# Loading one block in three smaller transfers at the moment when the first store joins a saturated load queue

## Chip, cores, metric

One core of one Trainium2 chip. The metric is device time in microseconds (us) of one execution, median over runs. The profiled span is about 1.7 us shorter than the time of the same run (316.3 against 318.03 for the kernel before).

## Reference

```python
# x: (8, 1024, 2048) float32, gamma: (2048,), eps: scalar
rms = np.sqrt(np.mean(x ** 2, axis=-1, keepdims=True) + eps)
out = gamma * x / rms
return out * (1 / (1 + np.exp(-out)))      # SiLU
```

The 8192 rows of 8 KB are read once and written once: 67.1 MB each way.

## The kernel before

Rows are taken in 16 blocks of 512. A block is a tile of 128 partitions with 4 rows (32 KB) each, so a block is one transfer of 128 contiguous runs of 32 KB. Loads go out on the SyncE queue (q1 in the profile), stores on the ScalarE queue (q10). There are six block buffers; block `b + 6` is loaded when the store of block `b` has landed.

```python
    def load(b):
        xt = pool.tile([P, J * d], f32, name="xt")          # J = 4 rows per partition
        nc.sync.dma_start(out=xt, in_=xb[b])
        blocks[b] = xt
    # ... sums: squares of two rows on ACT, of two on DVE; the store of an earlier
    # ... block is issued on ACT after the first of its squares
    def store(b):
        nc.scalar.dma_start(out=ob[b], in_=blocks[b])
        if b + LEAD < nblk:                                  # LEAD = 6
            load(b + LEAD)
    # ...
        grow = pool.tile([P, J * d], f32, name="xt")         # the sixth buffer, for gamma
        for b in range(BUFS - 1):                            # loads 0 to 4
            load(b)
        # ... constants, gamma load on the ScalarE queue, gamma broadcast by matmul
        load(BUFS - 1)                                       # load 5
        sums(0); invert(0); finish(0)
        sums(1); invert(1)
        for b in range(1, last - 1):
            sums(b + 1, after_first=[b - 1])                 # store b-1 goes out here
            finish(b)
            invert(b + 1)
        # ... the last block is stored in two halves
```

Of the kernel before, what the change touches and what calls it, by code (L numbers as in the profile page):

```python
# [1 line left out]

# [4 lines left out]

ACT = mybir.ActivationFunctionType
ALU = mybir.AluOpType


@with_exitstack
def kernel(
    ctx: ExitStack,
    tc: tile.TileContext,
    x: bass.AP,
    gamma: bass.AP,
    eps: bass.AP,
    out: bass.AP,
):  # L20





    nc = tc.nc
    P = nc.NUM_PARTITIONS
    f32 = mybir.dt.float32
    x2 = x.flatten_outer_dims()
    o2 = out.flatten_outer_dims()  # L30
    n, d = x2.shape
    J = 4
    BUFS, LEAD = 6, 6
    nblk = n // (P * J)
    xb = x2.rearrange("(b p j) d -> b p (j d)", p=P, j=J)
    ob = o2.rearrange("(b p j) d -> b p (j d)", p=P, j=J)

    singles = ctx.enter_context(tc.tile_pool(name="singles", bufs=1))
    pool = ctx.enter_context(tc.tile_pool(name="pool", bufs=BUFS))
    small = ctx.enter_context(tc.tile_pool(name="small", bufs=2))  # L40
    psum = ctx.enter_context(tc.tile_pool(name="psum", bufs=1, space=bass.MemoryType.PSUM))

    g = singles.tile([P, d], f32)
    eps_t = singles.tile([P, 1], f32)
    ones = singles.tile([P, P], f32)
    junk_a = psum.tile([P, d], f32, name="junk_a")
    junk_v = psum.tile([P, d], f32, name="junk_v")
    blocks, rmss, rstds = {}, {}, {}

    def load(b):  # L50
        xt = pool.tile([P, J * d], f32, name="xt")
        nc.sync.dma_start(out=xt, in_=xb[b])  # L52
        blocks[b] = xt

    def row(b, j):
        return blocks[b][:, j * d:(j + 1) * d]

    def sums(b, after_first=()):


        ss = small.tile([P, J], f32, name="ss")
        na = J // 2
        for j in range(na, J):
            nc.vector.tensor_tensor_reduce(  # L64
                out=junk_v, in0=row(b, j), in1=row(b, j), scale=1.0, scalar=0.0,
                op0=ALU.mult, op1=ALU.add, accum_out=ss[:, j:j + 1])
        for j in range(na):
            nc.scalar.activation(out=junk_a, in_=row(b, j), func=ACT.Square,  # L68
                                 accum_out=ss[:, j:j + 1])
            if j == 0:  # L70
                for s in after_first:
                    store(s)
        rms = small.tile([P, J], f32, name="rms")
        nc.scalar.activation(out=rms, in_=ss, func=ACT.Sqrt, scale=1.0 / d, bias=eps_t)  # L74
        rmss[b] = rms

    def invert(b):
        rstd = small.tile([P, J], f32, name="rstd")
        nc.vector.reciprocal(out=rstd, in_=rmss.pop(b))  # L79
        rstds[b] = rstd  # L80

    def finish(b, halves=False):
        for j in range(J):
            nc.vector.scalar_tensor_tensor(out=row(b, j), in0=row(b, j), scalar=rstds[b][:, j:j + 1],  # L84
                                           in1=g, op0=ALU.mult, op1=ALU.mult)
            if j % 2:
                cols = slice((j - 1) * d, (j + 1) * d)
                nc.scalar.activation(out=blocks[b][:, cols], in_=blocks[b][:, cols], func=ACT.Silu)  # L88
                if halves:
                    nc.scalar.dma_start(out=ob[b][:, cols], in_=blocks[b][:, cols])  # L90

    def store(b):
        nc.scalar.dma_start(out=ob[b], in_=blocks[b])  # L93
        if b + LEAD < nblk:
            load(b + LEAD)

    with tc.manual_schedule():


        Q = 4  # L100
        w = d // Q
        grow = pool.tile([P, J * d], f32, name="xt")
        for b in range(BUFS - 1):
            load(b)
        nc.vector.memset(ones, 1.0)  # L105
        nc.vector.memset(eps_t, float(eps))  # L106
        nc.scalar.activation(out=junk_a[:, 0:1], in_=ones[:, 0:1], func=ACT.Square)  # L107
        nc.scalar.dma_start(out=grow[0:P:P // Q, 0:w],
                            in_=bass.AP(tensor=gamma.tensor, offset=gamma.offset, ap=[[w, Q], [1, w]]))
        for c in range(Q):  # L110
            k = c * (P // Q)
            nc.tensor.matmul(junk_v[:, c * w:(c + 1) * w], ones[k:k + 1, :], grow[k:k + 1, 0:w],  # L112
                             start=True, stop=True)
        nc.vector.tensor_copy(out=g, in_=junk_v)  # L114
        load(BUFS - 1)


        last = nblk - 1
        sums(0)
        invert(0)  # L120
        finish(0)
        sums(1)
        invert(1)
        for b in range(1, last - 1):
            sums(b + 1, after_first=[b - 1])
            finish(b)
            invert(b + 1)
        store(last - 2)
        finish(last - 1)
        store(last - 1)  # L130
        sums(last)
        invert(last)
        finish(last, halves=True)


# [1 line left out]
_INS = ['x', 'gamma', 'eps']  # L137
_OUTS = [((8, 1024, 2048), 'float32')]

_NUMBERS = {'eps': 9.999999747378752e-06}  # L140


# [26 lines left out]
```

## Time and profile before

| | kernel before |
|---|---|
| time, median | 317.5 us (317.49 to 317.79, 3 runs) |
| DVE, ACT busy | 71%, 71% |
| load queue, store queue, share of 16 engines' time | 49.7%, 49.2% |
| 32 KB packet | 1.213 us |
| first load packet starts; last packet ends | 1.7 us; 314.9 us |

The transfer engines' row of the slices and the two queue shares say what binds here. The page, the table by stretches and the chain are quoted in the prediction.

A *packet* is one record of one transfer engine in the trace; here it is one contiguous run (32, 16 or 8 KB), and each transfer ends on each engine with a *landing packet* of 4 bytes, which counts its landing. The records don't name the engine, so I followed the packets by their times, each to the one that starts where it ends (16 chains per trace). The *loss at the join* is, per engine, what the time from one packet's start to the next exceeds the usual for its size, summed from 30 us to just after the first large store packet; figures are means over the 16 engines unless said otherwise.

All times below are counted from the start of the profiled span, as on the page and in the timeline. The packet times in the prediction and in the expectations are not: they are counted from a fixed point of the trace that lies 0.40 us ahead of the span's start in this profile. So 0.40 us is to be taken off the packet times there ("first store packet at 41.4 us", "ends at 313.76"). The losses are differences and are not touched by it. The expectations give some losses up to 0.07 us differently from the table, from an earlier count.

### The profile page before, as it was taken

How to read it: one execution, taken by the hardware profiler on the slowest of the kernel's cores; microseconds unless marked ns; L12 is line 12 of the kernel's file. 1: busy time of each engine (PE TensorE's matmuls, PEld its weight loads, DVE VectorE, ACT ScalarE, POOL GpSimd, SP SyncE). 2: the span in 40 equal slices, each digit the busy share in tenths (PEclk: the TensorE clock that was granted, in tenths of full speed). 3: DMA queues.
4: the chain of work that ended last, by engine and by line, in shares of the span. 5: the costliest groups of instructions: out<-in, count | busy, mean ns of one | idle time of the engine just before them, and what ended most of it. 6: DMA issues, size and time to landing. Idle time of an engine off the chain costs nothing.

```text
span 316.3 us, 444 instructions
## 1 busy us (share of the span) xinstructions
PE 2.1 (1%) x8; PEld 0.5 (0%) x8; DVE 223.5 (71%) x147; ACT 223.8 (71%) x144; POOL 0.2 (0%) x4
## 2 busy tenths in 40 slices
PE   0200000000000000000000000000000000000000
PEld 0000000000000000000000000000000000000000
DVE  0679499999493983939849397593966939993900
ACT  1357958999967777678676687676786776879540
POOL 0000000000000000000000000000000000000000
DMA  8999999999999999999999999999999999999996
GB/s 328 402 464 410 452 390 410 452 419 443 439 424 452 411 452 410 452 414 456 406 456 414 448 414 448 439 423 452 414 452 410 452 414 456 406 456 410 452 407 269
DMA packets 4763, 134.25 MB, mean 425 GB/s; under 512 B 532, under 2 KB 532, under 8 KB 536
## 3 DMA queue, kind: packets, MB, share of 16 engines
q1 hardware_dynamic: 2304, 67.11, 49.7%
q10 hardware_dynamic: 2456, 67.12, 49.2%
q14 instruction: 3, 0.02, 0.0%
HBM read 67.12 MB, written 67.11 MB: 424 GB/s over the span
## 4 chain that ended last, share of the span: by engine, by line
DMA 74%; DVE 14%; ACT 5%; issue 2%; DVEq 1%; ACTq 0%; SPq 0%
DMA xt<-in_x_dram 44%; DMA out_dram<-xt 30%; DVE xt L84 11%; ACT xt L88 3%; DVE junk_v L64 3%; ACT junk_a L68 1%; DVEq L164 1%; ACT L74 0%; ACT rms L74 0%; DVE rstd L79 0%; ACTq L93 0%; DVE ss L64 0%; SPq L52 0%; DVEq L64 0%; ACTq L74 0%
## 5 line engine op out<-in xcount | busy, mean ns | idle before, releaser
L84 DVE SCALAR_TENSOR_TENSOR xt<-xt,rstd,g 128x2048 f32<-128x2048 f32 x64 | 146.2, 2347 | 0.1
L88 ACT ACTIVATE xt<-xt 128x4096 f32<-128x4096 f32 x32 | 115.4, 3615 | 36.8 <-DVE xt L84 36.7
L64 DVE CUSTOM_DVE_ANT_0 junk_v<-xt 128x2048 f32<-128x2048 f32 x32 | 73.5, 2298 | 56.1 <-DMA xt<-in_x_dram 55.5
L68 ACT ACTIVATE junk_a<-xt 128x2048 f32<-128x2048 f32 x32 | 60.1, 1879 | 29.2 <-DMA xt<-in_x_dram 28.3
L74 ACT ACT_TABLE_LOAD x15 | 19.2, 1283 | 9.9 <-DVE ss L64 9.9
L88 ACT ACT_TABLE_LOAD x15 | 19.2, 1283 | 3.1 <-DVE xt L84 2.9
L79 DVE RECIPROCAL rstd<-rms 128x4 f32<-128x4 f32 x16 | 2.8, 172 | 11.3 <-ACT rms L74 11.3
L114 DVE COPY g<-junk_v 128x2048 f32<-128x2048 f32 x1 | 2.3, 2292 | 9.2 <-PE junk_v L112 9.2
L68 ACT ACTIVATION_READ_ACCUMULATOR junk_a<-xt 128x1 f32 x32 | 6.0, 186 | 0.0
L74 ACT ACTIVATE rms<-ss,eps_t 128x4 f32<-128x4 f32 x16 | 4.8, 297 | 1.2 <-DVE ss L64 1.1
L64 DVE DVE_READ_ACCUMULATOR2_ANT ss<- 128x1 f32 x32 | 4.5, 141 | 0.0
L112 PE MATMUL junk_v<-xt,ones 1*128 1x512 f32 x8 | 2.1, 1133 | 8.1 <-DMA xt<-in_gamma_dram 8.1
L107 ACT ACT_TABLE_LOAD x1 | 1.3, 1283 | 0.7 <-PEq L150 0.7
L105 DVE MEMSET ones<- 128x128 f32 x1 | 0.2, 165 | 0.8 <-PEq L150 0.8
L112 PEld LDWEIGHTS junk_v<-xt,ones 1*128 1x128 f32 x8 | 0.5, 306 | 8.1 <-issue 8.1
L107 ACT ACTIVATE junk_a<-ones 128x1 f32<-128x1 f32 x1 | 0.2, 174 | 0.0
L150 POOL MEMSET const-uint8-127<- 128x1 uint8 x1 | 0.1, 102 | 0.0
L150 POOL MEMSET const-bfloat16-1.0<- 128x1 bf16 x1 | 0.1, 101 | 0.0
L150 POOL MEMSET const-float32-0.0<- 128x1 f32 x1 | 0.1, 98 | 0.2 <-issue 0.2
L150 POOL MEMSET const-float32-1.0<- 128x1 f32 x1 | 0.1, 98 | 0.0
L106 DVE MEMSET eps_t<- 128x1 f32 x1 | 0.1, 59 | 0.0
## 6 DMA issues: line engine op xcount, KB each, us to landing
xt<-in_x_dram SPq DMA_DIRECT2D x16, 4096.0 KB, 42.0
out_dram<-xt ACTq DMA_DIRECT2D x15, 4096.0 KB, 35.2
out_dram<-xt ACTq DMA_DIRECT2D x2, 2048.0 KB, 10.4
xt<-in_gamma_dram ACTq DMA_DIRECT2D x1, 8.0 KB
```

The source lines that it names most:

```text
L64: nc.vector.tensor_tensor_reduce(out=junk_v, in0=row(b, j), in1=row(b, j), scale=1.0, scalar=0.0, op0=ALU.mult, op1=ALU.add, accum_out=ss[ ...
L68: nc.scalar.activation(out=junk_a, in_=row(b, j), func=ACT.Square, accum_out=ss[:, j:j + 1])
L74: nc.scalar.activation(out=rms, in_=ss, func=ACT.Sqrt, scale=1.0 / d, bias=eps_t)
L79: nc.vector.reciprocal(out=rstd, in_=rmss.pop(b))
L84: nc.vector.scalar_tensor_tensor(out=row(b, j), in0=row(b, j), scalar=rstds[b][:, j:j + 1], in1=g, op0=ALU.mult, op1=ALU.mult)
L88: nc.scalar.activation(out=blocks[b][:, cols], in_=blocks[b][:, cols], func=ACT.Silu)
L105: nc.vector.memset(ones, 1.0)
L107: nc.scalar.activation(out=junk_a[:, 0:1], in_=ones[:, 0:1], func=ACT.Square)
L112: nc.tensor.matmul(junk_v[:, c * w:(c + 1) * w], ones[k:k + 1, :], grow[k:k + 1, 0:w], start=True, stop=True)
L114: nc.vector.tensor_copy(out=g, in_=junk_v)
L150: nc = _bacc.Bacc("TRN2", target_bir_lowering=False, num_devices=1)
L164: with _tile.TileContext(nc) as tc:
```

## The change

The intent: when the first store (store 0, issued at 36.7 us) joins, the engines shall be working on 8 KB load packets instead of 32 KB ones, so that the store gets in sooner. Block 3 is the block in flight then.

```diff
-    def load(b):
+    def load(b, cuts=(0, 4)):
         xt = pool.tile([P, J * d], f32, name="xt")
-        nc.sync.dma_start(out=xt, in_=xb[b])
+        for c0, c1 in zip(cuts, cuts[1:]):
+            c = slice(c0 * d, c1 * d)
+            nc.sync.dma_start(out=xt[:, c], in_=xb[b][:, c])
         blocks[b] = xt
 ...
-        for b in range(BUFS - 1):
+        for b in range(3):
             load(b)
 ...     (constants and gamma load, unchanged)
+        load(3, cuts=(0, 2, 3, 4))
+        load(4)
```

## The prediction

> **What bounds the kernel now.** I read the busy shares first, then the slices and the queues, then the table by stretches, then the chain, and last the tail of the timeline.
>
> The page of the kernel before:
>
> ```profile
> span 316.3 us, 444 instructions
> PE 2.1 (1%) x8; PEld 0.5 (0%) x8; DVE 223.5 (71%) x147; ACT 223.8 (71%) x144; POOL 0.2 (0%) x4
> ...
> DMA  8999999999999999999999999999999999999996
> ...
> q1 hardware_dynamic: 2304, 67.11, 49.7%
> q10 hardware_dynamic: 2456, 67.12, 49.2%
> ```
>
> DVE and ACT are busy 71% of the span; the sixteen transfer engines are at 9 in every slice but the first and the last. The two queues (q1 loads, q10 stores) hold 49.7 + 49.2 = 98.9% of all engine time. A packet is a whole row of a block: 2304 packets of q1 are 16 loads x 128 rows of 32 KB plus 16 x 16 small ones that count the landing. So the kernel is bound by moving 134.2 MB, and only the remaining 1.1% or a better rate is to be won.
>
> The table by stretches shows where the rate falls short:
>
> ```profile
> 2.00:36.00 34.00, 2.09 (x8) 0.55 (x8) 20.95 (x14) 17.56 (x14) 0.00 (x0) 1.00 0.98 421
> 36.00:44.00 8.00, 0.00 (x0) 0.00 (x0) 5.70 (x6) 6.85 (x10) 0.00 (x0) 1.00 1.00 385
> 44.00:64.00 20.00, 0.00 (x0) 0.00 (x0) 19.97 (x13) 16.19 (x11) 0.00 (x0) 1.00 1.01 437
> 64.00:150.00 86.00, 0.00 (x0) 0.00 (x0) 64.15 (x44) 68.13 (x45) 0.00 (x0) 1.00 1.00 433
> 150.00:278.00 128.00, 0.00 (x0) 0.00 (x0) 94.61 (x61) 92.90 (x58) 0.00 (x0) 1.00 1.00 432
> ```
>
> The last two columns are the transfer engines' share and GB/s. From 64 us on the rate is 432 to 433 GB/s; in the 8 us in which the first store joins it is 385 although the engines count as fully busy: packets take longer there. I therefore went to the single packets of the trace. A 32 KB packet takes 1.213 us, load or store, nearly everywhere; on one engine packets follow each other without a gap, and load and store packets alternate strictly one by one whenever both queues have work. Two places stick out. The first packet of each engine, at 2.1 us, is 0.77 us too long on average. And around 38 to 42 us, after the first store is issued, one or two load packets of each engine are too long, together 0.85 us on average (0.55 at the least, 1.51 at the most), after which the first store packet follows at 41.2 to 43.3 us. All the rest of the run has 0.15 us of such excess on average. So the sum of the span is: 2.1 us until the first packet, (2048 + 2048) x 1.213 / 16 = 310.5 us of packets, 0.77 + 0.85 + 0.15 = 1.8 us of excess, which makes 314.4; the worst engine ends at 315.3 (it has the 1.51 us of excess at the join, and 1 us of other hiccups), most at 313.7; then about 1 us of ending.
>
> The chain and the timeline at the join and in the tail:
>
> ```profile
> 36.67 24.75 DMA out_dram<-xt
> ...
> 61.49 41.87 DMA xt<-in_x_dram
> ```
> ```profile
> 36.67 0.36 ACTq L93 DMA_DIRECT2D out_dram<-xt  x1
> ...
> 52.13 2.27 DVE L64 CUSTOM_DVE_ANT_0 junk_v<-xt 128x2048 f32<-128x2048 f32 x1
> ...
> 55.81 0.34 ACTq L93 DMA_DIRECT2D out_dram<-xt  x1
> ```
> ```profile
> 285.68 0.34 ACTq L93 DMA_DIRECT2D out_dram<-xt  x1
> ...
> 300.25 0.34 ACTq L90 DMA_DIRECT2D out_dram<-xt  x1
> ...
> 304.77 0.34 ACTq L90 DMA_DIRECT2D out_dram<-xt  x1
> ```
>
> The first store takes 24.75 us: about 4.5 until its first packet, 18.2 for eight packets per engine alternating with loads (7 x 2.426 + 1.213), and the landing. In the tail, the half stores are issued at 300.25 and 304.77 us, but the packets show the store before them running until about 304.3 us and the first half until about 309.1. So there is about 4 us of slack ahead of the last stores: the end is set by the transfers, and a microsecond won or lost anywhere in the transfers goes straight to the end.
>
> **What the Trainium skill says.** "DMA: Bandwidth & Descriptors", section "Queues, rings and completion order": each engine takes turns between the queues it has work for, packet by packet, draining a whole packet from one before switching. The trace agrees, with L, S, L, S at 1.213 us each; it differs in that a packet here is one descriptor of 32 KB, not some nine to seventeen descriptors. The same page, "Issuing engines are not separate DMA queues": transfers issued from different engines run on the same 16 engines and interleave; the 49.7% and 49.2% agree. The same page, "Where 436 GB/s comes from", gives 435 GB/s as the ceiling of the ports: the trace's 432 to 433 is at it, so no split of a transfer can raise the plateau.
>
> **The change part by part.**
> 1. Block 3 becomes a transfer of 16 KB rows and two of 8 KB rows. Each engine then has 8 packets of 16 KB and 16 of 8 KB instead of 8 of 32 KB. The two last stores have 16 KB packets of 0.611 us, against 1.213 for 32 KB: a fixed part of 0.009 us and 0.602 per 16 KB, hence, an estimate, 0.310 us for 8 KB. 24 packets instead of 8 cost 16 x 0.009 = 0.14 us per engine, and two more landing packets 0.02: **+0.16 us**, on the bound.
> 2. Two more issues on the load queue, 0.33 us each by the timeline's issue times; the queue is filled tens of us ahead: 0. The gamma load is written ahead of loads 3 and 4, but goes out on another queue, at the same place of ACT's order: 0.
> 3. The program uses eight landing semaphores in turn. With two more transfers ahead, load 5 must wait, besides for the release of its buffer (about 10 us), for load 1's landing (22.8 us) as it reuses its semaphore. Load 5's packets don't start until after 60 us: 0.
> 4. Which packets are under way at the join. Load 3 starts at 32.0 us: 8 x 0.611 = 4.9, so the 8 KB rows begin at 36.9, just when the store is issued (36.67), and alone would last until 41.9. The change is aimed well. The first store packets wait behind fewer bytes, so I expect them at 38.5 to 40.5 us instead of 41.3. From there the strict alternation gives the store 32 KB against 8 KB: a pair takes 1.213 + 0.310 = 1.52 us, eight pairs 12.2 us. The first store's packets end at about 51 to 52 us and it lands at 52 to 53.5, a landing 8 to 9 us earlier than at 61.4. Load 6 is issued that much earlier, but behind loads 4 and 5: no gain, since bytes moved per time are the same. Load 3 lands at 52 to 53 instead of 45; DVE wants it at 52.13, so it waits up to 1.5 us, which costs nothing as DVE is not the bound.
> 5. What the join costs. The excess of 0.85 us falls on load packets of 1.2 us. If it is a share of the packet in progress, 8 KB packets bring it to about a quarter, say -0.6 us; if it is a fixed delay of starting the store queue, it stays. I take **-0.3 us**.
> 6. A second join. Store 1 is issued at 55.8 us, because ACT comes to it only then, whatever store 0 does. The store queue, which in the kernel before is never empty after 41 us, now runs dry from about 52 to 60 us; loads have the engines alone, with 32 KB packets, and store 1 joins into those. If joining an empty queue costs 0.85 us each time, it is paid here in full; if only the first use of the queue costs, nothing. Half: **+0.4 us**.
> By 61 us the same bytes are moved in both kernels, load and store queues stand as before within a packet, and the steady part is the same. Sum: 0.16 - 0.3 + 0.4 = about +0.2 us, within the noise of 317.49 to 317.79: I predict 317.6 us.
>
> **Rivals.**
> - The split does what it is meant to: join excess gone to a quarter, also on the slowest engine (1.51 to 0.4), and the second join is free. For it: the long packets are exactly the 32 KB load packets before the first store packet. Then -0.6 to -1.1 + 0.16: 316.6 to 317.0 us.
> - The cost is moved, not removed: the first join as long as before or the second pays the same. For it: the start of the load queue at 2.1 us shows the same 0.77 us of excess without any other queue beside it, so it looks like the cost of starting a queue. Against: nothing in the trace shows a queue restarted. Then 317.7 to 318.6.
> - A new wait: the late landing of load 3 holds DVE, load 5 waits for load 1. Against: tens of us of slack in the load queue, and 29% idle DVE. Only if store 1's issue went far beyond 56 us and loads 4 and 5 ran out would the engines idle; two loads alone last 19 us, so no.
>
> **Range and chances.** The terms that can move the end are each under 1.1 us; 2% is 6.35 us. All of the run's losses together (2.1 at the start, 1.8 excess, the spread of the engines' ends) are less than that, so faster by 2% is nearly excluded, and slower would need engines idle for 6 us. The range 316.7 to 318.6 covers the first two rivals and the noise. Faster 0.01, within 2% 0.98, slower 0.01.
>
> **What would show it.** Step 1: 8 KB packets of about 0.31 us. Step 4: the first store's landing falls from 24.75 us to 16 or 17, load 6 is issued at about 53 us instead of 61.4, and load 3 lands after 51 us. Step 5: the sum of excess at 36 to 42 us against 0.85. Step 6: a stretch without store packets between 52 and 60 us, and long load packets at its end or none. Wrong it would be if the steady rate differed from 432, if the final stores were issued after the queue ran dry, or if a stretch in the middle had idle engines.

## The result

317.88 us median (317.81 to 318.19, 6 runs) against 317.56 us (317.38 to 317.85, 6 runs) for the kernel before; ratio 1.0011, 95% interval 0.9998 to 1.0024. A second comparison later gave 317.85 against 317.58, ratio 1.0013 (1.0000 to 1.0025). So it is the same within 2%, and most likely slower by 0.3 to 0.4 us, as the means of both comparisons say (0.34 and 0.37 us).

The page of the changed kernel:

```profile
span 316.4 us, 448 instructions
PE 2.1 (1%) x8; PEld 0.5 (0%) x8; DVE 223.6 (71%) x147; ACT 223.7 (71%) x144; POOL 0.2 (0%) x4
...
q1 hardware_dynamic: 2592, 67.11, 49.7%
q10 hardware_dynamic: 2456, 67.12, 49.2%
```

Only the number of load packets has changed, by 288: 2 x 128 more rows and 2 x 16 more landing packets. Little else on the page shows the change. The table by stretches of the changed kernel does (last column GB/s):

```profile
2.00:36.00 34.00, 2.09 (x8) 0.54 (x8) 20.95 (x14) 17.43 (x14) 0.00 (x0) 1.00 0.97 418
36.00:44.00 8.00, 0.00 (x0) 0.00 (x0) 5.58 (x6) 6.85 (x10) 0.00 (x0) 1.00 0.99 365
44.00:64.00 20.00, 0.00 (x0) 0.00 (x0) 19.97 (x13) 16.19 (x11) 0.00 (x0) 1.00 1.01 437
64.00:150.00 86.00, 0.00 (x0) 0.00 (x0) 63.38 (x43) 67.26 (x44) 0.00 (x0) 1.00 1.00 433
150.00:278.00 128.00, 0.00 (x0) 0.00 (x0) 94.35 (x61) 93.40 (x58) 0.00 (x0) 1.00 1.00 434
```

From 44 us on the rates are as before (437, 433, 434 against 437, 433, 432). In the stretch of the join the rate is 365 GB/s instead of 385: that stretch was meant to become better and became worse. The same stretch in the other profiles, two with the loads of block 3 whole (before_again, order_only) and two more of the changed kernel (after_again, after_timed), in this order:

```profile
36.00:44.00 8.00, 0.00 (x0) 0.00 (x0) 5.76 (x6) 6.85 (x10) 0.00 (x0) 1.00 1.00 393
36.00:44.00 8.00, 0.00 (x0) 0.00 (x0) 5.83 (x6) 6.85 (x10) 0.00 (x0) 1.00 0.98 393
36.00:44.00 8.00, 0.00 (x0) 0.00 (x0) 5.79 (x6) 6.85 (x10) 0.00 (x0) 1.00 1.00 375
36.00:44.00 8.00, 0.00 (x0) 0.00 (x0) 5.72 (x6) 6.85 (x10) 0.00 (x0) 1.00 1.00 378
```

A window this short is coarse, because a packet is counted as a whole, so here are the packets of one engine in each trace, worked out from the packet records (start:kind and KB(duration), L load, S store; landing packets left out, one of the load queue stands between the last two S32 of the first line):

```
before  37.66:L32(1.27) 38.93:L32(1.84) 40.76:S32(1.21) 41.97:L32(1.21) 43.18:S32(1.21) 44.40:S32(1.21)
after   38.28:L8(0.31) 38.59:L8(0.50) 39.09:L8(0.34) 39.42:L8(0.93) 40.34:L8(0.44) 40.78:L8(0.46)
        41.24:L8(0.40) 41.63:S32(1.21) 42.84:L8(0.31) 43.15:S32(1.21) 44.36:L8(0.31) 44.66:S32(1.21)
```

The 8 KB packets, otherwise 0.31 us, take 0.34 to 0.93 us for the 3 us ahead of the first store packet, and that packet comes no sooner (41.6 against 40.8 us). The alternation of 32 KB and 8 KB then takes place as meant, but on most engines only three or four 8 KB packets are left for it.

The timeline of the changed kernel, the store issues and the load that follows store 0:

```profile
36.79 0.36 ACTq L95 DMA_DIRECT2D out_dram<-xt  x1
...
55.94 0.34 ACTq L95 DMA_DIRECT2D out_dram<-xt  x1
...
61.49 19.72 SPq L54 DMA_DIRECT2D xt<-in_x_dram  x2
...
301.53 0.34 ACTq L92 DMA_DIRECT2D out_dram<-xt  x1
...
306.06 0.34 ACTq L92 DMA_DIRECT2D out_dram<-xt  x1
```

Load 6 goes out at 61.49 us, as before: in this run two engines were late at the join, had no 8 KB packets left, and finished store 0 at 61.1 us, although the median engine was through at 57.0. A transfer lands with its slowest engine. In the two later profiles of the same kernel no engine was as late, and load 6 went out at 56.47 us (after_again) and 57.81 us (after_timed):

```profile
56.47 0.33 SPq L54 DMA_DIRECT2D xt<-in_x_dram  x1
57.81 0.33 SPq L54 DMA_DIRECT2D xt<-in_x_dram  x1
```

That difference of 4 to 5 us did not reach the end. The two last half stores are issued 1.3 us later than before, with loads behind stores by 0.7 of a 32 KB packet per engine (by 250 us the loads have started 116.3 of their 128, instead of 117.0). The first packets of these stores start at 304.1 us on the median engine (303.9 on the earliest), without a gap before them on any engine, so there are still 2.3 us and more between issue and first packet; before, the median was 303.6. The delay of the join has travelled through the whole run: 0.6 us at the first large store packet and 0.5 us here, on the median engine.

The waits of the load queue's issuer, before and after:

```profile
SPq L52 <- DMA xt<-in_gamma_dram: 4.8, 1, 4.8
SPq L52 <- PE junk_v L112: 2.2, 1, 2.2
```
```profile
SPq L54 <- DMA xt<-in_x_dram: 18.7, 1, 18.7
```

This is the new wait that was foreseen: load 5 now waits 18.7 us for load 1's landing, for whose semaphore it is next in turn, where it waited for gamma and the matmuls before. It is issued at 23.0 us and its packets start at 64.6 us at the earliest, so the wait costs nothing.

### The profile page after: what moved, and what is told of

Read it like the earlier page. It is cut to its first block, busy times and chain, and to the rows that moved or that the text cites. A ratio compares the mean times of both kernels' runs of the same rounds, so it can differ in the third digit from the quotient of the medians.

```text
span 316.4 us, 448 instructions
## 1 busy us (share of the span) xinstructions
PE 2.1 (1%) x8; PEld 0.5 (0%) x8; DVE 223.6 (71%) x147; ACT 223.7 (71%) x144; POOL 0.2 (0%) x4
## 4 chain that ended last, share of the span: by engine, by line
DMA 74%; DVE 14%; ACT 5%; issue 2%; DVEq 1%; ACTq 0%; SPq 0%
DMA xt<-in_x_dram 45%; DMA out_dram<-xt 29%; DVE xt L86 11%; ACT xt L90 3%; DVE junk_v L66 3%; ACT junk_a L70 1%; DVEq L169 1%; ACT L76 0%; ACT rms L76 0%; DVE rstd L81 0%; ACTq L95 0%; DVE ss L66 0%; SPq L54 0%; DVEq L66 0%; ACTq L76 0%
```

## The experiments

**Theory A**: the join costs a fixed time while the store queue starts, whatever the load packets are. Sub-forms: A1, only at the first store of the run; A2, and E after it, each time the queue comes from idle. **Theory B**: smaller load packets let the store in sooner or cheaper (the change's intent, and my step 5). **Theory C**: each load packet that passes during the start loses something, so smaller ones make the join dearer. **Theory F**: the loss goes with the size of the store's first packet. **G**: the first large store packets pay, whatever went before. D is chance.

All twelve runs gave correct results. The table has the loss at the join (mean of 16 engines, and its range over the engines), the median over the engines of the start of the first large store packet and of the end of the last packet (us from the span's start), and the time. Single times are one run beside the kernel before.

| run | loads / first store at the join | loss us | engines | first large store packet | end | time, before beside it |
|---|---|---|---|---|---|---|
| kernel before | 32 KB / 32 KB | 0.86 | 0.65 to 1.51 | 40.97 | 313.36 | 317.56 |
| before_again | 32 / 32 | 0.76 | 0.41 to 1.39 | 40.91 | 313.27 | 317.36, 317.34 |
| order_only | 32 / 32 | 0.59 | 0.32 to 1.53 | 40.77 | 313.13 | 317.66, 317.65 |
| two_16k | 16 / 32 | 1.04 | 0.74 to 1.34 | 41.29 | 313.70 | 317.87, 317.65 |
| changed kernel | 8 / 32 | 1.15 | 0.83 to 1.59 | 41.59 | 313.82 | 317.88, 317.56 |
| after_again | 8 / 32 | 1.01 | 0.77 to 1.44 | 41.34 | 313.79 | 318.00, 317.34 |
| after_timed | 8 / 32 | 0.98 | 0.66 to 1.43 | 41.28 | 313.70 | 317.85, 317.58 |
| all_8k | 8 / 32 | 1.11 | 0.84 to 1.41 | 41.41 | 313.85 | 317.89, 317.34 |
| dry | 32 / 16 | 0.80 | 0.62 to 1.36 | 40.79 | 313.46 | 317.57, 317.65 |
| store_8k | 32 / 8 | 0.25 | 0.04 to 0.40 | 41.53 | 313.08 | 319.06, 317.65 |
| both_8k | 8 / 8 | 0.80 | 0.63 to 1.01 | 41.02 | 314.62 | 318.01, 317.58 |
| warm_store | 32 / 32, small store at 1 us | 0.53 | 0.37 to 0.65 | 50.57 | 313.28 | 317.63, 317.34 |
| tiny_ahead | 32 / 32, small store just ahead | 0.61 | 0.44 to 0.78 | 50.64 | 313.16 | 317.29, 317.58 |
| pre_store | 32 / 32, small store 8 us ahead | 1.09 | 0.60 to 1.73 | 42.48 | 313.50 | 317.86, 317.58 |

### before_again: how steady the figures are

No edit.

> The kernel before, unchanged, for a second profile: how far the figures of the join repeat. In the first profile the load packets around the first store's joining were too long by 0.85 us per engine on average (0.55 to 1.51), the first store packet came at 41.4 us (median of the engines), and the engines ended at 313.76 us (median). If these figures are steady, the second profile shows 0.75 to 0.95 us, 41.2 to 41.6 and 313.5 to 314.0. If they are noise, the difference of 0.85 to 1.1 us between the two kernels means nothing.

Loss 0.76 us, first large store packet 40.91 us, ends 313.27 us: inside what was expected, once 0.40 us is taken off the expected times. The order_only run below, the same transfers in the same order, gave 0.59, so the loss with 32 KB on both sides varies between 0.59 and 0.86 from profile to profile.

### after_again: the changed kernel once more

No edit.

> The changed kernel, unchanged, for a second profile. In the first, the engines lost 1.11 us on average at the join (long packets 1.06 and gaps 0.05), the first store packet came at 41.96 us (median) and the engines ended at 314.19 us (median). If smaller load packets make the join dearer, this shows 1.0 to 1.2 us again; if that was chance, it may come out at 0.85 as before.

Loss 1.01 us, ends 313.79 us. The dearer join repeats. With the profile of after_timed there are three for this kernel: 1.15, 1.01, 0.98.

### all_8k: block 3 entirely in 8 KB packets

```diff
-        load(3, cuts=(0, 2, 3, 4))
+        load(3, cuts=(0, 1, 2, 3, 4))
```

> Block 3 in four transfers of one row (8 KB packets throughout). Theory A, the join costs a fixed time for which the store queue starts, whatever the load packets are: loss at the join 1.0 to 1.2 us per engine as in the changed kernel, first store packet about 5 us after the store's issue (41.7 to 42.2 us), as the packets from 37 us on are the same 8 KB. Theory B, smaller packets ahead let the store in sooner or cheaper: a loss under 0.8 us or a first store packet before 41 us. In both, 8 KB load packets of 0.305 us and 0.03 us more per engine for the eight more packets.

Loss 1.11 us, first large store packet at 41.41 us. Theory B is refuted: with 8 KB packets ahead, the store comes in neither sooner nor cheaper. Counted from the issue of store 0 it comes later: after 4.6 to 4.8 us on the median engine in the four profiles with 8 KB loads, after 4.2 to 4.3 us in the three with 32 KB. The packets of 37 us and later are what counts, and they are the same in both kernels.

### warm_store: a small store at the very start

```diff
         nc.vector.memset(eps_t, float(eps))
+        nc.scalar.dma_start(out=ob[nblk - 1][:, 0:P], in_=ones)   # overwritten by the last store
```

> The kernel before with one small store (128 rows of 512 bytes, overwritten by the last block's store 300 us later, so the result stays right) ahead of the gamma load on the store queue. Theory A1, the cost at the join is that of the first store of the run (first use of the write path): long packets at the join fall from 0.85 to under 0.2 us, the first real store packet comes sooner (about 40.5), and the time falls by 0.5 to 1.0 us, to 316.5 to 317.0; part may be paid at the start instead. Theory A2, it is paid whenever stores join a queue of loads: 0.85 us as before, and the time 317.5 or a little more. Theory B (packet size): as A2.

A miss in part. The gamma load, behind the small store on the same queue, waited: the matmuls waited for it 18.1 us instead of 8.1, and all the compute began later; store 0 went out at 46.0 us. The loss at its join, just ahead of 50.6 us, was still 0.53 us, and the time 317.63 us (ratio 1.0008, interval 0.9994 to 1.0022). So the cost is not that of the run's first store as such: A1 fails in that form. No engine lost more than 0.65 us here, though, where 1.4 to 1.5 us was seen on single engines in the profiles above.

### two_16k: an intermediate size

```diff
-        load(3, cuts=(0, 2, 3, 4))
+        load(3, cuts=(0, 2, 4))
```

> Block 3 in two transfers of two rows (16 KB packets). So far the engines lost 0.85 and 0.75 us at the join with 32 KB load packets and 1.21, 1.07 and 1.18 us with 8 KB. Theory C, a loss that grows with the number of load packets that pass while the store queue starts: 16 KB lies between, 0.9 to 1.05 us, engines' ends 313.9 to 314.1. Theory D, only the chance of the run, or the landing packets between the parts: no order by size, so anything from 0.75 to 1.2.

Loss 1.04 us, above all the runs with 32 KB loads and a whole first store without a small one ahead (0.59 to 0.86), but not below all those with 8 KB (0.98 to 1.15). It speaks for C against B and D, yet does not show that the loss goes on growing from 16 to 8 KB.

### order_only: the moved lines alone

```diff
-        load(3, cuts=(0, 2, 3, 4))
+        load(3)
```

> The changed kernel with block 3 in one transfer: only the moved lines are left. All theories: join loss 0.7 to 0.9 us, first store packet at 41.4, ends 313.7 to 313.9, as before, since the order of the loads on their queue is the same. If the moved lines cost anything, the ends come later than 314.0.

Loss 0.59 us and 317.66 us beside 317.65: the moved lines cost nothing. The loss and the median end of 313.13 us are below what I expected (0.7 us, and 313.3 after taking off 0.40 us).

### dry: does a second join pay again?

```diff
     def store(b):
+        if b == 0:
+            nc.scalar.dma_start(out=ob[0][:, :2 * d], in_=blocks[0][:, :2 * d])
+            return
+        if b == 1:
+            nc.scalar.dma_start(out=ob[0][:, 2 * d:], in_=blocks[0][:, 2 * d:])
+            load(LEAD)
         nc.scalar.dma_start(out=ob[b], in_=blocks[b])
```

> The kernel before with the first store cut in two halves (16 KB packets), the second half going out with the second store: the store queue runs dry from about 46 to 60 us, and joins 32 KB loads a second time. Theory E, the loss is paid whenever stores join loads after the queue was idle: a second loss of 0.5 to 0.9 us per engine just ahead of the first store packet at about 60 us, and ends of 314.2 to 314.6. Theory A1, once per run: none there (under 0.1), ends as before, 313.7 to 313.9. The small early store of the last experiment, idle for 31 us before the real one, left 0.52 us, which speaks for E.

The experiment did not reach its aim: alternating with 32 KB loads, the first half lasted until 53 us, and the second went out at 52.07, so there was no store data for only 2.4 to 3.6 us, where the hand-over between two stores takes 2.4 us in the kernel before. No loss followed. Of the 0.80 us at the first join, 0.2 fell on the load packet after the first store packet. What the run left open the changed kernel itself answers in part: in its profiles most engines have no store data for 3.6 to 6.0 us at about 55 to 60 us (median engine 4.2, 4.8 and 4.8), 32 KB loads are under way, and store 1's packets come in at 59 to 60 us with no packet lengthened. Such a short dry spell cost nothing. But store 1 had been issued at 55.7 to 55.9 us, about when store 0's last packets passed on the median engine, so this is no long idle time; one after large stores was not tried.

### store_8k: small packets on the store's side

```diff
     def store(b):
-        nc.scalar.dma_start(out=ob[b], in_=blocks[b])
+        for c in range(J if b == 0 else 1):
+            cols = slice(c * d, (c + 1) * d) if b == 0 else slice(0, J * d)
+            nc.scalar.dma_start(out=ob[b][:, cols], in_=blocks[b][:, cols])
```

> The kernel before with the first store in four transfers of 8 KB rows, the loads whole: small packets on the store's side of the join. Theory F, the loss is the time in which the engines fetch the first store packets before they write any, so it goes with the size of the store's packet: it falls from 0.8 to 0.3 to 0.5 us. Theory A or E (a fixed cost of starting the queue): 0.7 to 0.9 us as before. In both the store then gets one 8 KB packet per 32 KB load packet, so it lands late, at 85 to 95 us.

Loss 0.25 us. The table by stretches of this run:

```profile
36.00:44.00 8.00, 0.00 (x0) 0.00 (x0) 5.60 (x6) 6.85 (x10) 0.00 (x0) 1.00 1.01 423
```

423 GB/s at the join is the best of the runs in which a whole store joins there. So this side of the join matters, as F says, as far as one profile shows it. But the kernel is slower, 319.06 us: the store lands late (load 6 goes out at 71.71 us instead of 61), the load queue runs dry from about 66 us to 76, and one engine loses 1.9 us after the join and ends at 315.9 us, while the median engine ends at 313.1.

### both_8k: small on both sides

The edit of store_8k, on the changed kernel.

> The changed kernel with the first store also in four transfers of 8 KB rows: small packets on both sides of the join. Measured so far: loss at the join 0.59 to 0.85 us with 32 KB on both sides, 1.07 to 1.21 us with small loads and 32 KB stores, 0.25 us with 32 KB loads and 8 KB stores. Theory F, the loss is about the time of one store packet that is fetched before any is written: 0.25 to 0.4 us here. Theory C, small load packets lose more of themselves: 0.9 to 1.2 us. In both the store gets as much as the loads, packet by packet, and the run is not slower than the changed kernel by more than 1 us, unless some engine falls behind as in the run with 8 KB stores alone (319.06).

Loss 0.80 us, between the two forecasts: above the 0.25 us of the same store with 32 KB loads, below the 0.98 to 1.15 us of the same loads with a 32 KB store. Neither F nor C alone gives it; it looks as if both sizes act, in opposite directions, with one profile each for the 8 KB stores. The engines then lose another 0.9 us at 84 to 88 us. The trace shows it on whole load packets around the place where store 1 ends and store 2 begins, both of 32 KB packets, with store 2 issued at 69.64 us. So a loss of this size can come at a later hand-over between two stores too; the others looked at, the first eight stores of every run, lose under 0.1 us, and why this one does not is open. The time is 318.01 us.

### tiny_ahead: 512 bytes per row ahead of the rest

```diff
     def store(b):
+        if b == 0:
+            nc.scalar.dma_start(out=ob[0][:, :P], in_=blocks[0][:, :P])
+        c0 = P if b == 0 else 0
-        nc.scalar.dma_start(out=ob[b], in_=blocks[b])
+        nc.scalar.dma_start(out=ob[b][:, c0:], in_=blocks[b][:, c0:])
```

> The kernel before with the first store cut into its first 512 bytes of each row and the rest (32256 bytes), issued one right after the other. Theory F in the form that only the first store packet of an engine counts: loss at the join under 0.3 us, since that packet is 512 bytes. Theory G, what counts is the first large packets fetched, or the start of the queue as such: 0.6 to 0.9 us as before.

The table by stretches of this run:

```profile
36.00:44.00 8.00, 0.00 (x0) 0.00 (x0) 5.89 (x6) 6.85 (x10) 0.00 (x0) 1.00 1.04 447
44.00:54.00 10.00, 0.00 (x0) 0.00 (x0) 10.00 (x6) 6.28 (x3) 0.00 (x0) 1.00 0.94 381
```

The small packets come in at 40.2 us and nothing is lost (447 GB/s); the loss, 0.61 us, comes at 47.5 to 50.8 us, right ahead of the first large store packet. That is G: at this join the loss belongs to the first large store packet, not to the start of the queue, and F in its narrow form is refuted.

### pre_store: the same small pieces 8 us earlier

The cut of tiny_ahead, with the 512-byte pieces issued after the first half of block 0 is done (at 28 us).

> The same cut, but the 512-byte pieces go out 8 us earlier (28.2 us, after the first half of block 0 is done), so that the store queue holds small packets from about 33 us until the rest joins behind them at 41 us. If the loss is that of a store queue coming from idle with a large packet (F): under 0.2 us at 33 us and under 0.3 us at 41 us, the engines' median end at 313.2 to 313.4 instead of 313.8 us, and the time 0.4 to 0.6 us under the kernel before. If every first large store packet pays (G): 0.6 to 0.9 us at about 41 us, and the time as before within 0.2 us.

A miss for F again. The small packets alternate with the loads from 32 us on at no loss, and then 1.09 us is lost from 39 us until the first large store packet (42.5 us on the median engine), when the large part joins behind them. The time, 317.86 us (ratio 1.0005, 0.9994 to 1.0017), is not below the kernel before. On 13 of the 16 engines the small packets were through, landing packet included, before the longest load packet began, just as in tiny_ahead; the packet sizes are the same too, and yet the loss is 1.09 against 0.61 us. What makes this difference is open. It also shows that a join with 32 KB loads can cost as much as one with 8 KB loads.

### after_timed: the changed kernel in more rounds

No edit.

> The changed kernel once more, timed against the kernel before in five rounds. If the dearer join (1.15 against 0.75 us, from five profiles) and 0.04 us of more packets set the difference: 0.3 to 0.5 us slower (ratio 1.001 to 1.0016), engines' median end 314.1 to 314.4. If the 0.32 us of the first comparison were noise: ratio within 1.0000 and 1.0005.

317.85 us (317.72 to 318.52, 6 runs) against 317.58 (317.22 to 318.22, 11 runs), ratio 1.0013, interval 1.0000 to 1.0025; ends 313.70 us. The second comparison agrees with the first.

No experiment pointed to a version that is faster than the kernel before by more than the noise: tiny_ahead had the lowest time, 317.29 us in its one run, but the kernel before had a run of 317.22.

## Why the prediction was right, and where it was right by luck

The time, 317.88 us against 317.6 forecast, and the verdict were right because the bound was: the transfers set the end, the plateau rate did not change, the time between the last stores' issue and their first packets (2.3 us left) took up the shifts of the issues, and all the losses together are far below 2%. By its own steps:

- Step 1 (more packets): +0.16 was forecast. From one packet's start to the next it is 1.209 us for 32 KB, 0.607 for 16 and 0.306 for 8, so 8 x 0.607 + 16 x 0.306 - 8 x 1.209 = +0.08, and two landing packets +0.01: **+0.09 us**. I had fitted the fixed part per packet to durations, which overlap by about 4 ns. For the same reason the prediction's sum of the span, 314.4 us, is 1.0 us too long (256 packets per engine).
- Steps 2 and 3 (issues, load 5's semaphore): 0, as shown by order_only and by the wait of 18.7 us that nothing followed.
- Step 4 (the store gets in sooner, 38.5 to 40.5 us): **failed**. The first large store packet came at 41.3 to 41.6 us, 4.6 to 4.8 us after its issue, against 4.2 to 4.3 us with 32 KB loads. I had taken the delay for one of packets queued ahead; smaller ones did not shorten it. So most 8 KB packets had passed before the store came, about four pairs were left instead of eight, and load 6 was issued 3.4 to 5 us earlier in two profiles and not at all in the first. The 24.75 us from which I started are also those of a late engine: the median one of the kernel before was through at 59.1 us. That the landing does not matter was right.
- Step 5 (the join, -0.3 us): **failed, with the wrong sign**. It measured 1.15, 1.01 and 0.98 us against 0.86, 0.76 and 0.59 with 32 KB (order_only counted in), means 1.05 and 0.74: **+0.31 us**. Neither a quarter of the loss nor an unchanged one, the two cases weighed there, was right: smaller load packets made it dearer.
- Step 6 (a second join, +0.4 us): the dry spell came, at 55 to 60 us and so 4 to 5 us long instead of 8, and it cost **0**.

The sum of the measured terms is 0.09 + 0.31 + 0 = +0.40 us, as against +0.2 forecast. The mean end of the engines moved by 0.41 us (313.95, 313.87 and 313.76 after; 313.54, 313.47 and 313.33 before), that of the median engine by 0.52, that of the last engine by 0.24, and the means of the times by 0.34 and 0.37 us. So the account closes for the mean, in which it is counted, but the forecast sum was close because two wrong terms, -0.3 and +0.4, nearly cancelled. Of the rivals, the first is refuted; of the second, "moved, not removed", the part that said the first join is not made cheaper holds and the part with the second join does not.

Three figures of the prediction don't hold by themselves. From 317.5 us its terms (0.16 - 0.3 + 0.4 = 0.26) lead to 317.8, not 317.6. Its slack of 4 us ahead of the last stores was 3.1 us at the least (300.25 to 303.37), as packets and issues were counted from different zeros. And its range begins at 316.7, above the 316.6 of its first rival.

Shown is where the loss falls (mostly the 3 us of load packets ahead of the first large store packet) and that small load packets do not reduce it (the seven profiles with 32 KB or 8 KB loads and a whole 32 KB store as the first do not overlap: 0.59 to 0.86 in three and 0.98 to 1.15 in four). That the store's packet size acts on it rests on one profile. What in the engines causes the loss is open, and so are the 1.09 us of pre_store, the second loss of both_8k, and whether a store queue idle for long after large stores pays again.

## What to carry to other kernels

Where the transfer engines are saturated from first to last packet, count the engine time that a change adds or removes; what lands sooner in the middle is worth nothing until a queue runs dry or the slack at the end is used up. Don't cut transfers so that a newly started queue meets smaller packets: here the first store packet came 4.6 to 4.8 us after its issue instead of 4.2 to 4.3, and the cut cost 0.09 us for the packets and about 0.3 us at the join. And check each term of a forecast by itself, since a right total can rest on two errors.

## What the Trainium skill lacked or had wrong

- "DMA: Bandwidth & Descriptors", section "Latency and other measured facts", gives about 600 ns to the first byte on this path. On idle engines the trace agrees: the first load's first packet starts 0.63 us after the end of its issue (1.10 to 1.73 us). What the page lacks is the delay beside a running load queue: the first store's first packet comes 4.2 to 4.8 us after the start of its issue on the median engine.
- The same page, "Queues, rings and completion order", has the turn-taking by packets, and the trace agrees; but a turn here is one contiguous run, of 32 KB as of 8 KB, not nine to seventeen descriptors. So the size of the run sets the share of each queue: 32 KB stores against 8 KB loads take turns of 1.21 and 0.31 us.
- No page has a cost for a store queue that joins running loads: 0.59 to 0.86 us per engine with 32 KB on both sides, 0.98 to 1.15 with 8 KB loads, 0.25 with 8 KB stores (one profile); nor that a gap of 3.6 to 6 us in the store data cost nothing in three profiles.
